# First projection of a two-layer hybrid encoder: x·r ahead, c and r in PSUM, other homes for some small work

## The chip, the cores and the metric

The kernel runs on one core of a Trainium2 chip. The metric is the device time of one execution in microseconds. Its engines are PE (matmul; PEld is its weight load), DVE (vector), ACT (scalar), POOL (GpSimd) and SP, which here only issues transfers.

## The reference

Batch 1, 512 positions, width 1024, two layers. Each layer is a token mixer with three groups of heads and then a gated MLP with a convolution of width 3. Everything is float32.

```python
for l in range(DEPTH):
    mod = jax.nn.silu(c) @ w_ada[l] + b_ada[l]
    sh_a, sc_a, gt_a, sh_f, sc_f, gt_f = [m[:, None, :] for m in jnp.split(mod, 6, axis=-1)]
    h = rms_norm(x, g_attn[l]) * (1.0 + sc_a) + sh_a
    x = x + gt_a * hybrid_mixer(h, w_in[l], diff_lambda[l], diff_subln[l], na_rpb[l], w_out[l], l)
    h = rms_norm(x, g_ffn[l]) * (1.0 + sc_f) + sh_f
    x = x + gt_f * conv_glu_ffn(h, w_up[l], conv_w[l], conv_b[l], w_down[l])
return rms_norm(x, g_final)
```

The mixer projects h to q, k and v for 4 differential heads (a softmax minus lambda times a second one), 6 dilated heads (three dilation patterns merged) and 6 heads of 2-D neighbourhood attention, with rope on the first two groups, and projects their outputs by w_out.

## The kernel before

x lies transposed: eight tiles of 128 features by 512 positions. For precision every matmul operand is split into a rounded part hi and a rest lo, and a product is three matmuls: hi·hi, lo (weight)·hi and hi·lo (`mm3`, L485 to L488). One such matmul is 128 x 128 by 512 columns.

**Weights** come in 110 units per layer, in the order of use. `emit_raw` (L323) loads one into a `raw` buffer (4 of them) on SP's queue; `emit_split` (L335) copies it to hi on ACT (L354) and takes lo = raw - hi on POOL or DVE (L355, L356). Three w slots hold split units (three more f slots in the MLP), so the split runs about one unit ahead of PE. `free_unit` gives a slot back and splits the next unit.

**Modulation.** Each column block of `mod` is one `ada_step` (L405): a 128 x 1024 block of w_ada times silu(c), which is copied to all partitions as `cb`, summed on DVE (L414), and for two of six groups a one-column product `gsc` = g·(1 + sc) (L421). 16 steps belong to the first projection, 24 run during layer 0's attention, the rest during its MLP.

**The start** (L201 to L232, L1297 to L1302): c arrives as two rows, silu on ACT, two matmuls against a row of ones, two copies to `cb`. x is loaded on SP. `Norm` squares x on ACT, sums seven squares on DVE (L447), and sums over partitions by eight one-column matmuls (L456); POOL takes the power (L461), four plus four small matmuls spread r over the partitions (L468).

**The first projection** is the generator `g0` (L500). For each of eight k-blocks it makes h (`make_h`, L472: x·r on DVE, L477; hi on ACT, L480; the affine step again on DVE, L481; lo on POOL in this place, L482), and then runs 18 matmuls into six PSUM banks (pr, pr, pr, pt, s, s). The same function serves the later normalised inputs.

**Attention** (`attention_phase`, L571). Rope pairs turn two banks into q and k parts (`rope_pair`, L587: four multiplications on DVE, then an add or subtraction, L606, a cast on ACT, L613, and lo, L618, these two on DVE or, where `G` is passed, on POOL), which go through DRAM scratch to be stacked. `proj()` (L774) is a generator that emits the remaining projections: V of the differential heads (`vd`), V of the dilated heads (`vb`), further q/k pairs, V of the third group, then w_out. `v_rows` (L664) and `v_split` (L702) write one bank per 128 positions, copy hi on ACT and take lo on DVE (L710), after which the bank is free. The main loop (L1106) takes one piece of `proj()`, advances a clock that runs due stages in order, and starts attention steps where their buffers are free; this sets the order in which instructions are emitted, and each engine works its list in order (a scheduler may move an instruction that is ready earlier). A differential step: scores, row maximum (L927), two exponentials (L935), reciprocal (L941), coefficient (L942), difference (L943), four transposes (L833), hi (L837) and lo (L841). A neighbourhood step scales its probabilities in L1031. w_out is split in two groups of units, o1 and o2.

**The MLP** (`ffn_phase`, L1137) is a long run of matmuls on the same weight machinery; its `Norm` adds squares on POOL.

PSUM has eight banks, 2 KB per partition each: pr 3, s 2, pt 2, o 1.

Of the kernel before, what the change touches and what calls it, by code (L numbers as in the profile page):

```python
# [176 lines left out]
def build(ctx, tc, a):  # L177
# [321 lines left out]

    def g0(l, kind, norm, rb0, A_off, sh_g):  # L500
        h = []
        first = l == 0 and kind == "g0"
        rb = {0: rb0}

        def mk(k, half):
            if half != 1:
# [1 line left out]
            if first and half != 1:
                with tc.issue_after(norm.last.ins):
                    ada_step()  # L510
                ada_step()
                if wst["raw"] < 8:
                    emit_raw()
                else:
                    wst["auto"] = True
# [854 lines left out]
```

## Time and profile before

| | us |
|---|---|
| median of 3 runs | 1367.7 (1364.79 to 1368.34) |
| the profiled execution | 1369.17 |
| its span, first to last instruction | 1367.4 |
| PE busy | 1290.9 (94%) |
| DVE busy | 918.2 (67%) |
| ACT busy | 607.3 (44%) |
| POOL busy | 178.1 (13%) |

In the profile, busy time is what an engine's instructions cover; a busy PE may still run its matmuls at half clock, so the granted clock is read beside it. Times in rows count from the first instruction. "L356" is line 356 of the kernel. In a group, the last part is the idle time of the engine ahead of the group's instructions and what ended it.

### The profile page before, as it was taken

The numbers are of one execution on the slowest core, as the hardware profiler recorded it, in microseconds if no ns is written. First come the engines' busy times: TensorE is split into PE (matmuls) and PEld (weight loads), VectorE is DVE, ScalarE is ACT, GpSimd is POOL, SyncE is SP. The second block draws the span as 40 slices with busy tenths as digits, with TensorE's granted clock in tenths as the row PEclk, the third lists the DMA queues.
The fourth block names the chain that finished last, engine by engine and source line by source line (L and its number), as shares of the span: only waits on it lengthen the run. The fifth ranks groups of instructions, "written<-read, shape, count | busy, mean of one in ns | idle before, by whom it ended". The sixth has DMA issues, their size and how long they took to land.

```text
span 1367.4 us, 18510 instructions
## 1 busy us (share of the span) xinstructions
PE 1290.9 (94%) x6860; PEld 1101.6 (81%) x6860; DVE 918.2 (67%) x1689; ACT 607.3 (44%) x1069; POOL 178.1 (13%) x116
## 2 busy tenths in 40 slices
PE   5887899897999999999999889999999999999997
PEld 4686689776988888888899867988898888888886
DVE  7968987797686666756666599579766434443443
ACT  3236578564443133313343467786645312331331
POOL 3732321003000000000022232200300000000002
PEclk9999999999999999999999999999999999999998
DMA  9556577755365656665532655475333233333211
GB/s 354 192 172 156 161 231 215 198 174 158 113 190 181 209 175 192 186 203 171 164 114 90 192 142 163 125 194 149 109 99 118 93 97 99 96 93 93 84 40 62
DMA packets 74861, 206.76 MB, mean 151 GB/s; under 512 B 8594, under 2 KB 12562, under 8 KB 74644
## 3 DMA queue, kind: packets, MB, share of 16 engines
q1 hardware_dynamic: 74048, 203.72, 49.7%
q10 hardware_dynamic: 724, 1.87, 0.4%
q8 instruction: 54, 0.88, 0.3%
q14 instruction: 35, 0.29, 0.1%
HBM read 180.39 MB, written 15.73 MB: 143 GB/s over the span
## 4 chain that ended last, share of the span: by engine, by line
PE 72%; DVE 14%; DMA 5%; ACT 3%; issue 3%; POOL 2%; SPq 0%; POOLq 0%; DVEq 0%; ACTq 0%
PE pr L488 10%; PE pr L487 9%; PE pr L486 9%; PE s L487 5%; PE s L486 5%; PE s L488 5%; PE pt L488 4%; PE pt L487 4%; PE pt L486 4%; PE o L487 2%; PE o L486 2%; PE o L488 2%; PE pt L833 2%; DMA raw<-w 2%; DVE tmp L414 2%
## 5 line engine op out<-in xcount | busy, mean ns | idle before, releaser
L354 ACT CAST whi<-raw 128x1024 fp32r<-128x1024 f32 (+2 forms) x144 | 134.8, 937 | 261.7 <-PE pr L488 97.3
L356 DVE TENSOR_TENSOR wlo<-raw,whi 128x1024 fp32r<-128x1024 f32 (+2 forms) x101 | 110.5, 1094 | 94.0 <-ACT whi L354 93.3
L447 POOL TENSOR_TENSOR tmp<-tmp,tmp 128x256 f32<-128x256 f32 (+1 forms) x38 | 36.6, 966 | 881.4 <-ACT tmp L445 880.4
L414 DVE CUSTOM_DVE_ANT_0 tmp<-raw,cb,par 128x1024 bf16<-128x1024 f32 x80 | 108.5, 1356 | 51.2 <-DMA raw<-w_ada 50.6
L354 ACT CAST fhi<-raw 128x1024 fp32r<-128x1024 f32 (+1 forms) x76 | 74.6, 985 | 143.6 <-PE pr L488 53.6
L488 PE MATMUL pr<-h,whi 128*128 128x512 f32 (+1 forms) x330 | 121.9, 374 | 8.2 <-POOL h L482 7.6
L356 POOL TENSOR_TENSOR wlo<-raw,whi 128x768 fp32r<-128x768 f32 (+1 forms) x43 | 97.2, 2266 | 232.1 <-ACT whi L354 190.3
L486 PE MATMUL pr<-h,whi 128*128 128x512 f32 (+1 forms) x330 | 124.0, 376 | 1.9 <-DVE tmp L599 1.0
L487 PE MATMUL pr<-h,wlo 128*128 128x512 f32 (+1 forms) x330 | 122.8, 373 | 1.3 <-POOL wlo L356 1.3
L356 DVE TENSOR_TENSOR flo<-raw,fhi 128x1024 fp32r<-128x1024 f32 (+1 forms) x76 | 87.0, 1147 | 54.6 <-ACT fhi L354 53.7
L486 PE MATMUL pr<-h,fhi 128*128 128x512 f32 (+1 forms) x244 | 86.8, 357 | 0.7 <-ACT h L480 0.7
L487 PE MATMUL pr<-h,flo 128*128 128x512 f32 (+1 forms) x244 | 86.4, 356 | 0.0
L488 PE MATMUL pr<-h,fhi 128*128 128x512 f32 (+1 forms) x244 | 85.6, 357 | 0.4 <-DVE h L482 0.4
L488 PEld LDWEIGHTS pr<-h,whi 128*128 128x128 f32 x330 | 62.1, 190 | 20.4 <-POOL h L482 10.3
L486 PEld LDWEIGHTS pr<-h,whi 128*128 128x128 f32 x330 | 62.8, 190 | 12.2 <-DVE tmp L599 1.7
L487 PEld LDWEIGHTS pr<-h,wlo 128*128 128x128 f32 x330 | 62.9, 191 | 10.5 <-POOL wlo L356 1.7
L1192 ACT ACTIVATE tmp<-tmp 128x512 f32<-128x512 f32 x44 | 27.6, 631 | 95.4 <-DVE tmp L1187 77.5
L927 DVE TENSOR_REDUCE sm<-s 128x1 f32<-128x512 f32 x64 | 43.0, 681 | 31.0 <-PE s L925 30.6
L837 ACT CAST ph<-pt 128x512 fp32r<-128x512 f32 x80 | 46.5, 582 | 35.8 <-PE pt L833 35.2
L841 DVE TENSOR_TENSOR pl<-pt,ph 128x512 fp32r<-128x512 f32 x80 | 54.2, 683 | 11.9 <-ACT ph L837 11.7
L833 PE MATMUL pt<-cst,tmp 128*128 128x128 f32 x320 | 48.9, 276 | 12.9 <-DVE tmp L943 9.5
L480 ACT ACTIVATE h<-tmp,mod,gsc 128x256 fp32r<-128x256 f32 (+1 forms) x58 | 34.8, 620 | 55.4 <-DVE tmp L477 54.6
(264 smaller groups left out, 3652.4 us busy)
## 6 DMA issues: line engine op xcount, KB each, us to landing
raw<-w SPq DMA_DIRECT2D x132, 512.0 KB
raw<-w_ada SPq DMA_DIRECT2D x80, 512.0 KB
raw<-w SPq DMA_DIRECT2D x72, 384.0 KB
araw<-w_ada SPq DMA_DIRECT2D x16, 512.0 KB
raw<-w SPq DMA_DIRECT2D x16, 320.0 KB
scr0b<-nat SPq DMA_DIRECT2D x12, 256.0 KB
qs<-nat SPq DMA_DIRECT2D x24, 128.0 KB
ks<-nat SPq DMA_DIRECT2D x24, 128.0 KB
```

What stands on the lines that cost most here:

```text
L354: A.copy(hi, r)
L356: (G if on_pool else V).tensor_tensor(out=lo, in0=r, in1=hi.bitcast(F32), op=ALU.subtract)
L414: V.tensor_tensor_reduce(out=junk, in0=r, in1=cb, op0=ALU.mult, op1=ALU.add, scale=1.0, scalar=par[:, OFF_B + l * 48 + j:OFF_B + l * 48 + ...
L447: self.last = self.eng.tensor_tensor(out=self.sq[0][:, sl], in0=self.sq[0][:, sl], in1=self.sq[m][:, sl], op=ALU.add)
L480: ins = A.activation(out=hi, in_=t, func=AF.Identity, scale=A_col, bias=sh_col)
L486: PE.matmul(out, wh, hh, start=first, stop=False)
L487: PE.matmul(out, wl, hh, start=False, stop=False)
L488: return PE.matmul(out, wh, hl, start=False, stop=last)
L833: PE.transpose(pt[:, kt], P[:, kt * 128:kt * 128 + 128], ident)
L837: A.copy(st["ph", half][:, :, sl], pt)
L841: V.tensor_tensor(out=st["pl", half][:, :, sl], in0=st["pt", qb], in1=st["ph", half][:, :, sl].bitcast(F32), op=ALU.subtract)
L927: V.tensor_reduce(out=nm[:, m:m + 1], in_=s, axis=AX.X, op=ALU.max, negate=True)
```

## The change

It has eight parts.

1. c comes by one broadcast transfer on ACT's queue; two Silu make `cx` (in PSUM, two banks) and `cb` (in SBUF). The first 16 `ada_step` read `cx`.
2. The first projection gets a generator of its own, `first_g0`. The transfers of ten w_ada blocks and five w_in units are issued first. The squares are all on ACT, five adds on DVE, three squares go to the statistics matmuls. r is spread into one bank, and x·r is one 512-wide DVE operation per block, for all blocks ahead of the matmuls. Both affine passes of h are on ACT, both lo parts on POOL. Matmuls run pass by pass over the banks (hi·hi for all, then the weight's lo, then h's lo). The sixth bank is the one that holds r.
3. `gsc` is made on ACT (Identity with scale and bias g).
4. V of the differential heads takes two PSUM banks of 512 columns for four position blocks; copy and lo are done once per bank. In layer 0 both are pt banks, and the fourth bank of the projection is o instead of pt.
5. Rope pairs b0, b1 and b2 do their add and lo on POOL.
6. The lo parts of o1 and o2, and of the first w_in unit, are on POOL.
7. The difference coefficient is one `tensor_scalar` with two scalar operands.
8. The neighbourhood steps scale on ACT.

```diff
+    cest = ExitStack()
+    cpp = cest.enter_context(tc.tile_pool(name="cpp", bufs=1, space=PSUM))
...
-    crow = [tmp((1, 512)) for _ in range(2)]
-    orow = tmp((1, 128))
-    V.memset(orow, 1.0)
-    for i in range(2):
-        A.dma_start(crow[i], a["c"][:, i * 512:i * 512 + 512])
+    cx = cpp.tile([128, D], F32, name="cx")
+    A.dma_start(cb, a["c"].broadcast_to([128, D]))
...
-    for i in range(2):
-        A.activation(out=crow[i], in_=crow[i], func=AF.Silu)
-        b = ps("s")
-        PE.matmul(b, orow, crow[i], start=True, stop=True)
-        A.copy(cb[:, i * 512:i * 512 + 512], b)
+    A.activation(out=cx, in_=cb, func=AF.Silu)
+    A.activation(out=cb, in_=cb, func=AF.Silu)
...
-        r = wp.tile([128, n], F32, tag="raw", bufs=4, name=f"raw{uid()}")
+        if l == 0 and u < 8:
+            r = fpool["p"].tile([128, n], F32, tag="graw", bufs=8, name=f"graw{uid()}")
+        else:
+            r = wp.tile([128, n], F32, tag="raw", bufs=4, name=f"raw{uid()}")
...
-        on_pool = (l == 0 and 0 < u < 8) or kind in ("b", "cq", "ck", "vc", "vb")
+        on_pool = (l == 0 and u < 8) or kind in ("b", "cq", "ck", "vc", "vb", "o1", "o2")
...
+        cv = cx if ada_st["n"] < 16 else cb
...
-            V.scalar_tensor_tensor(out=gsc[l][:, o + k:o + k + 1], in0=mod[l][:, j:j + 1], scalar=1.0,
-                                   in1=par[:, base + l * 8 + k:base + l * 8 + k + 1],
-                                   op0=ALU.add, op1=ALU.mult)
+            g = par[:, base + l * 8 + k:base + l * 8 + k + 1]
+            A.activation(out=gsc[l][:, o + k:o + k + 1], in_=mod[l][:, j:j + 1], func=AF.Identity, scale=g, bias=g)
...
+    def first_g0():
+        fp = fpool["p"]
+        for _ in range(5):
+            ada_load()
+            ada_load()
+            emit_raw()
+        sq = []
+        for k in range(KD):
+            sq.append(fp.tile([128, S], F32, tag="xt", bufs=8, name=f"xq{k}"))
+            A.activation(out=sq[k], in_=x[k], func=AF.Square)
+            if k in (2, 4, 5, 6, 7):
+                V.tensor_tensor(out=sq[0], in0=sq[0], in1=sq[k], op=ALU.add)
+        st = ps("s", (128, 4))
+        todo = [(k, j) for k in (1, 3, 0) for j in range(4)]
+        for i, (k, j) in enumerate(todo):
+            PE.matmul(st[:, j:j + 1], sq[k][:, j * 128:j * 128 + 128], ones, start=(i == 0), stop=(i == len(todo) - 1))
...
+        G.tensor_tensor(out=r, in0=v, in1=mh[:, 0:4], op=ALU.pow)
+        rb = ps("s")
+        for j in range(4):
+            PE.matmul(rb[:, j * 128:j * 128 + 128], r[:, j:j + 1].to_broadcast([128, 128]), ident, start=True, stop=True)
...
+        def norm_x(k):
+            xt.append(fp.tile([128, S], F32, tag="xt", bufs=8, name=f"xt{k}"))
+            V.tensor_tensor(out=xt[k], in0=x[k], in1=rb, op=ALU.mult)
+
+        def mk(k):
+            if wst["raw"] < 8:
+                emit_raw()
+            t = xt[k]
+            emit_split()
...
+            ins = A.activation(out=hi, in_=t, func=AF.Identity, scale=sc, bias=sh)
+            t2 = tmp()
+            A.activation(out=t2, in_=t, func=AF.Identity, scale=sc, bias=sh)
+            G.tensor_tensor(out=lo, in0=t2, in1=hi.bitcast(F32), op=ALU.subtract)
...
+        ada_step()
+        ada_step()
+        norm_x(0)
+        norm_x(1)
+        mk(0)
+        norm_x(2)
+        norm_x(3)
+        ada_step()
+        ada_step()
+        mk(1)
+        for k in range(4, KD):
+            norm_x(k)
+        banks = yield
...
+        def mms(k, cs):
+            wh, wl = us[k]
+            for w, m in ((wh, 0), (wl, 0), (wh, 1)):
+                for c in cs:
+                    PE.matmul(banks[c], w[:, c * 128:c * 128 + 128], h[k][m], start=(k == 0 and w is wh and m == 0),
+                              stop=(k == KD - 1 and m == 1))
+
+        for k in range(KD):
+            if k + 2 < KD:
+                ada_step()
+                ada_step()
+                mk(k + 2)
+            us[k] = next_unit(("g0", k))
+            if k == 0:
+                mms(0, range(5))
+            elif k == 1:
+                mms(1, range(5))
+                mms(0, (5,))
+                mms(1, (5,))
+                free_unit()
+            else:
+                mms(k, range(6))
+            if k:
+                free_unit()
+            ck.step()
+        cest.close()
+        late["pt"] = ctx.enter_context(tc.tile_pool(name="ppt", bufs=1, space=PSUM))
+        yield h
...
-        banks = [take(t) for t in ("pr", "pr", "pr", "pt", "s", "s")]
+        t3 = "pt" if l else "o"
+        banks = [take(t) for t in ("pr", "pr", "pr", t3, "s", "s")]
...
-                tags = ("pt", "o", "pr", "pr")
+                tags = ("pt", "pt", "o" if l else "pt", "o" if l else "pt")
...
+                if k == 0 and nu == 2 and tb % 2:
+                    outs[tb] = outs[tb - 1][:, n:2 * n]
...
-                rope_pair(("b", p), bk[0], bk[1], ("pr", "pr"), 1)
+                rope_pair(("b", p), bk[0], bk[1], ("pr", "pr"), 1, G)
...
-                V.scalar_tensor_tensor(out=r, in0=r, scalar=ld, in1=lamv[l][0], op0=ALU.mult, op1=ALU.mult)
+                V.tensor_scalar(out=r, in0=r, scalar1=ld, scalar2=lamv[l][0], op0=ALU.mult, op1=ALU.mult)
...
-                    V.tensor_scalar(out=P[:, cols[i]], in0=P[:, cols[i]], scalar1=dn[:, i:i + 1], scalar2=None,
-                                    op0=ALU.mult)
+                    A.activation(out=P[:, cols[i]], in_=P[:, cols[i]], func=AF.Copy, scale=dn[:, i:i + 1])
...
-        ck.after(2, lambda: rope_pair(("d", 1), banks[2], banks[3], ("pr", "pt"), 0, G))
-        ck.after(4, lambda: rope_pair(("b", 0), banks[4], banks[5], ("s", "s"), 1))
+        ck.after(2, lambda: rope_pair(("d", 1), banks[2], banks[3], ("pr", t3), 0, G))
+        ck.after(4, lambda: rope_pair(("b", 0), banks[4], banks[5], ("s", "s"), 1, G))
```

## Rows read from the trace of the kernel before

**Rows 1.** table by stretch: length, busy us per engine (instructions), clock, DMA share, GB/s

```profile
10.00:20.00 10.00, 3.94 (x16) 3.56 (x16) 6.60 (x12) 2.50 (x5) 2.06 (x1) 1.00 1.03 411
...
66.90:96.67 29.77, 24.51 (x157) 23.82 (x157) 19.84 (x30) 9.63 (x17) 13.64 (x8) 0.89 0.54 164
...
96.67:200.00 103.33, 90.95 (x483) 72.82 (x483) 93.30 (x179) 66.60 (x143) 28.36 (x12) 1.00 0.65 182
...
260.00:345.00 85.00, 70.79 (x421) 61.23 (x422) 73.23 (x192) 41.11 (x93) 11.54 (x13) 0.94 0.59 177
...
345.00:741.00 396.00, 395.59 (x2039) 337.34 (x2039) 261.90 (x403) 134.80 (x181) 11.15 (x10) 1.00 0.54 165
...
771.00:860.00 89.00, 81.67 (x439) 68.04 (x438) 77.58 (x153) 62.15 (x134) 24.46 (x12) 0.98 0.59 165
```

**Rows 2.** timeline, 10 to 21 us: start, length, engine, line [idle before, releaser]

```profile
10.78 0.69 DVE L443 TENSOR_TENSOR tmp<-x 128x512 f32<-128x512 f32 x1 [0.93 <-DMA x<-x]
...
13.65 1.86 PE L456 MATMUL pt<-cst,tmp 128*128 128x1 f32 x8 [3.84 <-DVE tmp L447]
...
20.27 0.58 PE L486 MATMUL pr<-h,whi 128*128 128x256 f32 x1 [0.29 <-ACT h L480]
```

**Rows 3.** chain of waits, 20 to 67 us: shares by line, one PE step

```profile
by line: POOL h L482 24.4%; POOL wlo L356 19.6%; DVE tmp L414 19.0%; issue 6.2%; PE pr L488 4.1%; ACT whi L354 4.0%; DVE tmp L477 3.7%; DVE tmp L481 2.9%; DVE gsc L421 2.9%; DVE tmp L599 2.7%; PE s L488 2.0%; PE s L487 1.9%; PE s L486 1.4%;
...
52.26 0.23 PE pr L487
```

**Rows 4.** single lines, whole span: ns min/median/max, first and last start

```profile
L482 POOL TENSOR_TENSOR h<-tmp,h x10: 722/1767/2349, 22.0 to 62.2; 128x512 fp32r<-128x512 f32 x6, 128x256 fp32r<-128x256 f32 x4
...
L356 POOL TENSOR_TENSOR wlo<-raw,whi x43: 1802/2387/2834, 23.5 to 893.7; 128x768 fp32r<-128x768 f32 x23, 128x1024 fp32r<-128x1024 f32 x20
...
L414 DVE CUSTOM_DVE_ANT_0 tmp<-araw,cb,par x16: 1271/1443/2919, 13.5 to 56.6; 128x1024 bf16<-128x1024 f32 x16
...
L481 DVE TENSOR_SCALAR tmp<-tmp,gsc,mod x58: 400/408/2064, 21.6 to 1008.3; 128x256 f32<-128x256 f32 x52, 128x512 f32<-128x512 f32 x6
...
L942 DVE SCALAR_TENSOR_TENSOR sm<-sm,sm,nl x32: 200/210/2392, 100.5 to 837.8; 128x1 f32<-128x1 f32 x32
```

**Rows 5.** groups by form, ACT, 20 to 67 us: busy us, mean ns

```profile
L480 ACT ACTIVATE h<-tmp,mod,gsc 128x512 fp32r<-128x512 f32 x6 | 4.9, 814 | 23.9 <-DVE tmp L477 23.9
```

**Rows 6.** timeline of PE, the two stages behind the first projections

```profile
86.25 0.69 PE L687 MATMUL pr<-whi,h 128*128 128x384 f32 x1 [3.87 <-DVE va L710]
...
760.48 0.69 PE L687 MATMUL pr<-whi,h 128*128 128x384 f32 x1 [3.86 <-DVE va L710]
```

**Rows 7.** timeline of POOL in layer 0's V stage

```profile
73.19 1.29 POOL L606 TENSOR_TENSOR tmp<-tmp,tmp 128x512 f32<-128x512 f32 x1
...
74.44 3.47 POOL L618 TENSOR_TENSOR nat<-tmp,nat 128x512 fp32r<-128x512 f32 x2
...
81.24 3.81 POOL L356 TENSOR_TENSOR wlo<-raw,whi 128x768 fp32r<-128x768 f32 x2 [3.33 <-ACT whi L354]
```

**Rows 8.** timeline, one differential step, 132 to 136 us

```profile
132.04 2.38 POOL L356 TENSOR_TENSOR wlo<-raw,whi 128x1024 fp32r<-128x1024 f32 x1 [11.33 <-DMA raw<-w]
...
132.26 2.17 DVE L942 SCALAR_TENSOR_TENSOR sm<-sm,sm,nl 128x1 f32<-128x1 f32 x1
...
134.47 0.75 DVE L943 SCALAR_TENSOR_TENSOR tmp<-tmp,sm,tmp 128x512 f32<-128x512 f32 x1
...
135.37 0.63 PE L833 MATMUL pt<-cst,tmp 128*128 128x128 f32 x4 [1.90 <-DVE tmp L943]
```

**Rows 9.** groups of DVE: first row 96 to 200 us, the others 250 to 345

```profile
L942 DVE SCALAR_TENSOR_TENSOR sm<-sm,sm,nl 128x1 f32<-128x1 f32 x16 | 10.5, 657 | 0.2
...
L1031 DVE TENSOR_SCALAR tmp<-tmp,sm 128x256 f32<-128x256 f32 (+1 forms) x24 | 7.0, 329 | 0.1
...
L356 DVE TENSOR_TENSOR wlo<-raw,whi 128x640 fp32r<-128x640 f32 (+1 forms) x12 | 10.9, 911 | 0.2 <-ACT whi L354 0.2
```

**Rows 10.** waits of PE, 200 to 345 us: total us, times, longest

```profile
PE pt L456 <- POOL tmp L447: 3.0, 1, 3.0
```

More of the change, by code (lines that the diff above doesn't have):

```diff
@@ L413, in ada_step @@
         junk = tmp((128, D), BF16)
-        V.tensor_tensor_reduce(out=junk, in0=r, in1=cb, op0=ALU.mult, op1=ALU.add, scale=1.0,
+        V.tensor_tensor_reduce(out=junk, in0=r, in1=cv, op0=ALU.mult, op1=ALU.add, scale=1.0,
                                scalar=par[:, OFF_B + l * 48 + j:OFF_B + l * 48 + j + 1],
@@ L498, in proj_cols @@
                 yield
+    def first_g0():
[14 more added lines that the diff above has]
+            PE.matmul(st[:, j:j + 1], sq[k][:, j * 128:j * 128 + 128], ones, start=(i == 0), stop=(i == len(todo) - 1))
+        v = tmp((128, 4), tag="sm4", bufs=4)
+        V.tensor_scalar(out=v, in0=st, scalar1=1.0 / D, scalar2=EPS, op0=ALU.mult, op1=ALU.add)
+        r = tmp((128, 4), tag="sm4", bufs=4)
+        G.tensor_tensor(out=r, in0=v, in1=mh[:, 0:4], op=ALU.pow)
+        rb = ps("s")
+        for j in range(4):
+            PE.matmul(rb[:, j * 128:j * 128 + 128], r[:, j:j + 1].to_broadcast([128, 128]), ident, start=True, stop=True)
+        xt, h = [], []
+        def norm_x(k):
[6 more added lines that the diff above has]
+            emit_split()
+            if k >= 1:
+                wst["auto"] = True
+            sc, sh = gsc[0][:, k:k + 1], mods(0, 0)[:, k:k + 1]
+            hi, lo = [wp.tile([128, S], F32R, tag="h", bufs=16, name=f"h{uid()}") for _ in range(2)]
+            h.append((hi, lo))
+            ins = A.activation(out=hi, in_=t, func=AF.Identity, scale=sc, bias=sh)
+            t2 = tmp()
+            A.activation(out=t2, in_=t, func=AF.Identity, scale=sc, bias=sh)
+            G.tensor_tensor(out=lo, in0=t2, in1=hi.bitcast(F32), op=ALU.subtract)
+            if k == 5:
+                with tc.issue_after(ins.ins):
+                    late_consts()
+        ada_step()
[11 more added lines that the diff above has]
+        banks = yield
+        us = {}
+        def mms(k, cs):
[25 more added lines that the diff above has]
+        yield h
@@ L507, in mk @@
                 h.append([wp.tile([128, S], F32R, tag="h", bufs=16, name=f"h{uid()}") for _ in range(2)])
[L508 to L515, printed above, removed]
-            ins = make_h(rb, k, half, gsc[l][:, A_off + k:A_off + k + 1], mods(l, sh_g)[:, k:k + 1], h[k],
-                         G if first else V)
-            if first and k == 5:
-                with tc.issue_after(ins.ins):
-                    late_consts()
-        if first:
-            seq = [(k, half) for k in range(2) for half in range(2)] + [(k, 2) for k in range(2, KD)]
-        else:
-            seq = sorted([(k + half * 3.5, k, half) for k in range(KD) for half in range(2)])
-            seq = [(k, half) for _, k, half in seq]
+            make_h(rb, k, half, gsc[l][:, A_off + k:A_off + k + 1], mods(l, sh_g)[:, k:k + 1], h[k], V)
+        seq = sorted([(k + half * 3.5, k, half) for k in range(KD) for half in range(2)])
+        seq = [(k, half) for _, k, half in seq]
         made = 0
@@ L535, in ahead @@
                 made += 1
-        if first:
-            for _ in range(3):
-                ada_load()
-                ada_load()
-                emit_raw()
-            emit_split()
-            emit_split()
-        ahead(1 if not first else 2)
+        ahead(1)
         banks = yield
@@ L548, in g0 @@
         for i, (k, half) in enumerate(seq):
-            if not first and i == 1:
+            if i == 1:
                 with tc.issue_after(ins.ins):
@@ L1295, in ffn_phase @@
         return norm, rb0, fest
-    norm = Norm(V, (0,))
     fest = open_f("s")
-    for m in range(KD):
-        norm.add(m, on_v=m == 7)
-    norm.stats(2)
-    rb0 = start_g0(0, "g0", norm, norm.bcast(0), 0, 0)
+    rb0 = first_g0()
+    next(rb0)
     for l in range(DEPTH):
```

37 lines of the change are left out of this document (21 added, 16 removed).

## The prediction

> **What bounds the kernel now.** Read first the table by stretch [rows 1]. In the middle (345 to 741 us, gate and up projections and the first down blocks) PE is busy 395.59 of 396 us: nothing this change does can shorten that work. What can go is idle time of PE, and it lies in five places: the first 67 us; the V projection behind it (granted clock 0.89, so PE also worked part of it at 1.2 instead of 2.4 GHz); the differential and first dilated steps (96.67 to 200 us, PE busy 90.95 of 103.33); the end of attention (260 to 345 us, 70.79 of 85); and layer 1's copy of the second and third place (771 to 860 us, 81.67 of 89).
>
> Next the chain of waits from 20 to 67 us [rows 3]. The projection's own work is 8 k-blocks x 6 banks x 3 = 144 matmuls, and one takes 0.23 us where PE runs without waiting: 33.1 us. It lasts from 20.27 [rows 2] to 66.9, where the stretch of V begins [rows 1]: 13.5 us are waits. The chain gives them to POOL (h L482 and wlo L356) and DVE (L414): PE's first line has 4.1%. The spread of single durations says why [rows 4]: the same POOL subtraction takes 1.80 or 2.83 us, L414 1.27 or 2.92, and L481, with one SBUF input, 0.40 or 2.06. DVE and POOL hold each other up when both read SBUF.
>
> **The change part by part.** *Before the first matmul.* The two rows of c, two K=1 matmuls and two copies go; c comes as one 0.52 MB broadcast on ACT's queue ahead of par and cst. At the 411 GB/s that 10 to 20 us show [rows 1] it costs the eight x loads beside it 1.3 us (0 to 2.6). SP then holds ten w_ada and five w_in loads instead of six and three; they stand behind x, so x loses nothing. Behind the last x, 13.65 - 10.78 = 2.9 us of DVE work become a Square on ACT and one add, about 1.3; of the twelve statistics matmuls only four wait for the last add, where eight did (1.86 us, so 0.9); the power on POOL and the broadcast of r stay; the first h block is 512 wide, not 256 (+0.5). Sum: 1.3 - 1.6 - 0.9 + 0.5 = -0.7. ACT could be later than x: it has two 1024-wide Silu (at most 3.3 us, four times the 0.81 of a 512-wide ACT operation [rows 5]) and eight Squares to do. I take the first matmul at 20 us (18.5 to 21.5).
>
> *The projection.* c now stands in PSUM, x·r reads PSUM, the affine step leaves DVE for a second ACT pass (0.81 us), and the tiny gain product leaves for ACT. DVE then runs nothing with two SBUF inputs and no tensor_scalar here, so its 16 L414 should take their shortest time, and so should POOL. Per k: POOL 1.80 + 1.3 (L482's shortest is 0.72 at 256 columns, its 512 columns go by L356's rate) = 3.1; DVE 2 x 1.27 + 0.16 = 2.7; ACT three passes, 2.6; DMA 1.44 MB at 411 GB/s, 3.5; PE 18 x 0.23 = 4.1. PE becomes the bound. The new order is hi·hi for all banks, then lo, so lo is due 1.1 us or more after hi. Two waits are added: bank 6 holds r, so it starts behind block 1; and DVE does x·r for four blocks ahead of w_ada rows 2 and 3 and four more ahead of rows 4 and 5, behind which ACT's h of blocks 1 and 2 waits. By that order h of block 2 is there at about 30.2 us where PE is free at 29.5. With 33.1 us of work, about 1 us for starting at 1.2 GHz and 1 us for this wait, the end is 20 + 35.1 = 55: **12 us** earlier than 66.9. Lower bound: if POOL kept its longest durations, 2.83 + 2.35 = 5.2 per k, 20 + 2 + 8 x 5.2 = 63.6, a gain of 3. Upper: first matmul at 18.5 and no wait, 14.
>
> *Diff V in two banks.* In layer 0 PE waited 3.87 us at 86.25 for a V subtraction on DVE to give a pr bank back; in layer 1 3.86 us [rows 6]. V now takes both pt banks (layer 1: pt and o), so the three pr banks come free with rope's four multiplications, long before. Layer 0 also spent 29.77 x 0.11 x 2 = 6.5 us at 1.2 GHz, where a matmul takes twice as long: 0 to 3.3 us of work, I take 1.7. So 5.6 us can go in layer 0 and, with a wait of the same length, as much in layer 1. Against that, rope pair b0 moves its two adds and two subtractions to POOL: 2 x 1.29 + 2 x 1.74 = 6.1 us [rows 7]. They stand in POOL's queue ahead of the lo of V-b units 1 and 2 (81.24 us), which PE needs some 4 us into V-b; POOL was idle 3.3 us there, so the lo comes 0 to 2.8 us later and PE waits 0 to 3.3. And the next stage is paced by DVE (93.30 of 103.33 us busy [rows 1]), so not all of what PE gains is kept. I take 3 us in layer 0 (0 to 7.2) and 2 in layer 1 (the same ends).
>
> *Difference coefficient.* In 96.67 to 200 us L942 costs 10.5 us for 16 one-element operations [rows 9]; at its median of 0.21 [rows 4] it would be 3.4, so 7 us are spent behind POOL. The pattern [rows 8]: POOL's subtraction (wlo) starts at 132.04, L942 at 132.26, both end at 134.4, and PE gets its transposes 1.90 us late. But L943 follows at once (134.47), depends on L942 and reads two SBUF tiles. Without the wait at L942 it meets the same subtraction: the wait moves one instruction down. Only where other DVE work stands between is time won. I count 2 of the 7 us in layer 0 (0 to 7) and 1 in layer 1.
>
> The form L942 is given has no row. Bounds: 0.2, and what a wider tensor_scalar shows when POOL is in the way, 2.06 [rows 4]; I take 0.2, since one element is nearer to L942's own short times. The Trainium skill (SBUF — State Buffer, "Who interferes with whom") says that tensor_scalar in a two-port mode takes the pair that DVE shares with POOL, and that whichever starts first keeps it for the whole instruction. L481's 2.06 agrees; by that rule the new form may wait as the old one did, these 3 us would be 0, and the time 1348.
>
> *b1 and b2 on POOL.* Two more pairs move in this stage: DVE loses 8 operations as wide as L943 (0.75 us [rows 8]), 6 us. POOL gains 2 x 6.1 = 12 us in the same 103, and each time it meets a DVE operation with two SBUF inputs, L943 or L414, one of the two waits. I take 1 us in layer 0 (-3 to 4), 1 in layer 1. Queued behind a POOL subtraction that waits for ACT's cast or for a store to free its buffer is the lo of the next weight unit, and behind that PE; the lead is one unit, 24 x 0.23 = 5.5 us.
>
> *Scaling on ACT, o1 and o2 lo on POOL.* DVE loses 24 L1031 (7.0 us) and 12 lo parts (10.9 us) per layer [rows 9]. In 260 to 345 us DVE is busy 73.23 of 85, but PE's longest explained wait there is for POOL's norm adds, 3.0 us [rows 10]. ACT gains 24 operations of 256 columns, 0.4 to 0.8 us each (half and all of the 512-wide 0.81 [rows 5]), 10 to 19 us beside 41 busy: hidden. POOL was busy 11.54: it takes 12 x 1.5 to 1.8 = 20 us, hidden behind 5 x 3 x 0.23 = 3.4 us of PE per unit, except o2, whose lo is 0.9 us slower and holds its raw buffer longer. I take 1 us in all (-5 to 6).
>
> **Sum.** 12 + 3 + 2 + 2 + 1 + 1 + 1 + 1 = 23 us. The profiled execution took 1369.2 us (span 1367.4): 1346.2; the median stands 1.5 us lower, so **1345**.
>
> **Rivals.** *Start only.* POOL takes back in attention what DVE loses (wait moved to L943, b0 ahead of V-b's lo). For it: [rows 7, 8]. Against: POOL is busy 28 of the 103 us up to 200 [rows 1]. Time: 1367.7 - 12 = 1356.
> *Start half.* The broadcast holds x up and ACT's ten operations come late, so that the first matmul is at 23, and x·r ahead of w_ada costs 3 us more: gain 6, with 5 of the rest 1357, alone 1362. Against: the last x, 2.1 MB in all, was there at 10.78 us, 200 GB/s on the mean, half of the 411 shown behind it; there is room for c.
> *Slower: POOL's queue.* Each rope pair puts 6.1 us ahead of a lo that PE needs. It decides from where POOL is behind by more than the 5.5 us lead: 6.1 is just over. If all six pairs cost PE 3 us, half clock after each stall 1, and o2 2 per layer, that is 28 against 12 + 8: 1376. Against: POOL has idle time ahead of most lo parts.
> *Nothing changes.* Only if DMA, not POOL, paced the projection; 1.44 MB per k at 411 GB/s is 3.5 us, under PE's 4.1. No chance of weight.
>
> **How the numbers follow.** Forecast 1345 (1335 to 1354): 0.52. Start only, 1354 to 1361: 0.24. Start half, 1356 to 1362: 0.12. More than forecast, under 1335 (the good ends are 14 + 7 + 7 + 7 + 4 + 6 against the 12 + 3 + 2 + 2 + 1 + 1 taken): 0.05. Slower, over 1368: 0.07, of which a part ends within 0.3%. The range 1333 to 1361 leaves out 0.2 at most. 0.3% (4 us) is about what a measurement of this kernel can tell from no change: faster 0.87, same 0.07, slower 0.06.
>
> **What would show it.** Right: L414 all near 1.28 before 55 us; POOL's two subtractions near 1.8 and 1.3; last matmul of the first projection near 55; no PE wait on a V subtraction in either layer; L942 all near 0.2, some L943 over 2. Wrong: POOL wlo ahead of PE in the V stage with over 3 us; the first matmul after 22; PE's idle time at 260 to 345 us grown; rope on POOL waiting for buffers with a lo behind it.

## The result, and the profile after

| kernel | median us | range | ratio to the kernel before, same chip (95% interval) |
|---|---|---|---|
| before | 1368.02 | 1364.79 to 1369.39 | |
| after | 1352.79 | 1349.55 to 1354.78 | 0.9887 (0.9866 to 0.9908) |
| forecast | 1345 | 1333 to 1361 | 0.983 |

The change made the kernel 15.2 us faster where 23 were forecast (1345, against the 1352.79 measured). The profiled execution of after took 1349.55 us (span 1347.8), the lowest of its range, that of before 1369.17, near the highest of its own; so the two differ by 19.6 us, and some 4 us of that are chance.

To see where the time went, both traces are cut at the same places of PE's own work: the cuts of before are those of [rows 1], 20.27 us (first matmul of the projection, [rows 2]) and 66.9 (where the V stage begins), and each cut of after is the moment at which PE has done the same amount of matmul work, added up from the trace's matmuls (to 0.4 us).

| stretch | before us | after us | gain | forecast |
|---|---|---|---|---|
| to the first matmul | 20.27 | 24.19 | -3.9 | 0.3 |
| first projection | 46.63 | 34.96 | 11.7 | 11.5 |
| V, layer 0 | 29.77 | 27.15 | 2.6 | 3 |
| differential and first dilated steps | 103.33 | 99.83 | 3.5 | 3 |
| rest of attention, layer 0 | 145.0 | 141.02 | 4.0 | about 1 |
| gate, up, first down blocks | 396.0 | 395.97 | 0.0 | 0 |
| V and steps, layer 1 | 119.0 | 114.35 | 4.7 | 4 |
| next 80 us, layer 1 | 80.0 | 79.57 | 0.4 | 0 |
| end of attention, layer 1 | 70.0 | 74.03 | -4.0 | 0 |
| to the end | 357.4 | 356.73 | 0.7 | 0 |

The kernel after, by these stretches (the columns are those of [rows 1]):

```profile
0.00:24.19 24.19, 7.53 (x33) 7.06 (x33) 7.90 (x17) 10.57 (x17) 5.24 (x7) 1.00 0.91 342
24.19:59.15 34.96, 34.96 (x147) 28.83 (x148) 23.76 (x39) 20.17 (x31) 21.17 (x14) 1.00 0.80 307
59.15:86.30 27.15, 24.07 (x158) 23.50 (x156) 15.22 (x25) 9.25 (x15) 18.17 (x12) 0.94 0.54 166
86.30:186.13 99.83, 89.51 (x483) 73.51 (x483) 85.03 (x171) 65.99 (x142) 38.55 (x20) 1.00 0.69 189
186.13:327.15 141.02, 130.35 (x787) 115.26 (x786) 107.94 (x266) 100.64 (x227) 40.87 (x29) 0.96 0.68 195
327.15:723.12 395.97, 395.56 (x2039) 337.59 (x2039) 260.70 (x387) 140.72 (x197) 11.14 (x10) 1.00 0.54 165
723.12:837.47 114.35, 105.70 (x606) 90.76 (x605) 83.67 (x165) 70.69 (x148) 54.10 (x32) 0.99 0.61 173
917.04:991.07 74.03, 69.80 (x468) 63.42 (x467) 55.25 (x128) 45.52 (x92) 23.31 (x20) 0.95 0.31 93
```

PE is busy for all 34.96 us of the projection: it became the bound, as forecast. Its first nine matmuls start 0.43 us apart and the others 0.23. In the steps behind V, DVE fell to 85.03 us from the 93.30 of [rows 1] and POOL rose to 38.55 from 28.36, yet PE's idle time fell only from 12.4 to 10.3 us.

*Ahead of the first matmul.* Timeline of after, columns as in [rows 2]:

```profile
11.10 1.40 SPq L403 DMA_DIRECT2D araw<-w_ada  x2
...
13.46 1.28 DVE L416 CUSTOM_DVE_ANT_0 tmp<-araw,cx,par 128x1024 bf16<-128x1024 f32 x1 [1.56 <-DMA araw<-w_ada]
...
14.67 0.69 DVE L512 TENSOR_TENSOR xq<-xq,xq 128x512 f32<-128x512 f32 x1
...
15.27 1.27 DVE L416 CUSTOM_DVE_ANT_0 tmp<-araw,cx,par 128x1024 bf16<-128x1024 f32 x1
...
16.47 0.69 DVE L512 TENSOR_TENSOR xq<-xq,xq 128x512 f32<-128x512 f32 x1
...
17.21 1.87 PE L516 MATMUL s<-cst,xq 128*128 128x1 f32 x8 [4.77 <-DVE xq L512]
...
24.19 1.65 PE L567 MATMUL pr<-h,whi 128*128 128x512 f32 x3 [1.69 <-ACT h L540]
```

DVE waits 1.56 us for a row of w_ada, with the last two adds of the statistics (L512) queued behind that product and the next. PE sits idle for 4.77 us before it can finish the statistics, and all that follows comes late with them.

*In the projection.* Single lines of after, 20 to 64 us (ns min/median/max, first and last start):

```profile
L416 DVE CUSTOM_DVE_ANT_0 tmp<-araw,cx,par x14: 1275/1278/1280, 24.9 to 43.0; 128x1024 bf16<-128x1024 f32 x14
L357 POOL TENSOR_TENSOR wlo<-graw,whi x7: 1832/1862/1877, 20.3 to 47.7; 128x768 fp32r<-128x768 f32 x7
L543 POOL TENSOR_TENSOR h<-tmp,h x8: 1283/1297/1311, 24.9 to 54.2; 128x512 fp32r<-128x512 f32 x8
```

None varies any more: 1.28, 1.86 and 1.30 us, where [rows 4] showed 1.27 to 2.92 and 1.80 to 2.83.

*In V of layer 0.* The waits for a V subtraction [rows 6] are gone; two others stand there (timeline of after):

```profile
71.56 0.62 ACT L683 CAST nat<-tmp 128x512 fp32r<-128x512 f32 x1 [3.59 <-POOL tmp L676]
...
73.45 1.28 ACT L249 ACT_TABLE_LOAD   x1
...
74.95 0.56 ACT L783 CAST va<-pt 128x512 fp32r<-128x512 f32 x1
...
75.41 2.30 ACT L355 CAST whi<-raw 128x768 fp32r<-128x768 f32 x3
...
76.30 0.44 PE L760 MATMUL pr<-whi,h 128*128 128x384 f32 x1 [1.63 <-ACT whi L355]
76.32 5.38 POOL L357 TENSOR_TENSOR wlo<-raw,whi 128x768 fp32r<-128x768 f32 x3 [1.06 <-DMA scr0d<-nat]
...
78.18 0.44 PE L761 MATMUL pr<-wlo,h 128*128 128x384 f32 x1 [1.45 <-POOL wlo L357]
```

PE waits first for ACT's cast of V-b's second weight unit, which stands in ACT's queue behind the casts of rope pair b0, the first of which had waited 3.59 us for POOL's sum, and behind a table load of 1.28 us; and then for POOL's lo.

*In the steps.* Timeline of after at 793 us (layer 1):

```profile
793.58 2.83 POOL L357 TENSOR_TENSOR wlo<-raw,whi 128x1024 fp32r<-128x1024 f32 x1
...
796.37 1.25 POOL L676 TENSOR_TENSOR tmp<-tmp,tmp 128x512 f32<-128x512 f32 x1
...
797.66 0.62 ACT L683 CAST nat<-tmp 128x512 fp32r<-128x512 f32 x1 [3.39 <-POOL tmp L676]
798.18 0.58 ACT L913 CAST ph<-pt 128x512 fp32r<-128x512 f32 x1
...
798.82 0.74 PE L930 MATMUL o<-ph,va 128*128 128x256 f32 x4 [2.72 <-ACT ph L913]
```

This chain is the new one of the kernel after: a rope sum on POOL stands behind a weight lo, ACT's cast of that sum waits 3.39 us for it, and the cast of the probabilities (ph), which depends on nothing there, stands behind that cast, and PE behind ph. Layer 0 has a like one at 136 us, where the sum takes 2.25 us beside a w_ada product of DVE instead of standing behind a lo, and PE waits 2.09 us for ph.

### The profile page after: what moved, and what is told of

It is laid out like the page before. It is cut to its first block, busy times and chain, and to the rows that moved or that the text cites. A ratio compares the mean times of both kernels' runs of the same rounds, so it can differ in the third digit from the quotient of the medians.

```text
span 1347.8 us, 18449 instructions
## 1 busy us (share of the span) xinstructions
PE 1285.7 (95%) x6836; PEld 1102.7 (82%) x6836; DVE 849.0 (63%) x1534; ACT 639.8 (47%) x1150; POOL 240.0 (18%) x163
## 4 chain that ended last, share of the span: by engine, by line
PE 72%; DMA 9%; DVE 7%; POOL 4%; issue 4%; ACT 3%; SPq 1%; POOLq 0%; DVEq 0%; ACTq 0%
PE pr L489 9%; PE pr L488 9%; PE pr L487 9%; PE s L488 5%; PE s L487 5%; PE s L489 5%; PE pt L488 4%; PE pt L489 4%; PE pt L487 4%; PE o L488 2%; PE o L489 2%; PE o L487 2%; PE pt L909 2%; DMA raw<-w 1%; PE pr L567 1%
## 5 line engine op out<-in xcount | busy, mean ns | idle before, releaser
L355 ACT CAST whi<-raw 128x1024 fp32r<-128x1024 f32 (+2 forms) x136 | 128.1, 943 | 229.6 <-PE pr L489 78.2
L357 POOL TENSOR_TENSOR wlo<-raw,whi 128x768 fp32r<-128x768 f32 (+2 forms) x58 | 115.0, 1988 | 299.4 <-ACT whi L355 275.4
L357 DVE TENSOR_TENSOR wlo<-raw,whi 128x1024 fp32r<-128x1024 f32 (+1 forms) x78 | 90.8, 1164 | 101.4 <-ACT whi L355 100.6
L487 PE MATMUL pr<-h,whi 128*128 128x512 f32 (+1 forms) x300 | 113.2, 378 | 0.4 <-DVE tmp L669 0.4
L489 PE MATMUL pr<-h,whi 128*128 128x512 f32 (+1 forms) x300 | 111.5, 372 | 0.4 <-DVE h L483 0.4
L488 PE MATMUL pr<-h,wlo 128*128 128x512 f32 (+1 forms) x300 | 111.7, 372 | 0.0
L917 DVE TENSOR_TENSOR pl<-pt,ph 128x512 fp32r<-128x512 f32 x80 | 54.6, 685 | 18.0 <-ACT ph L913 17.7
L489 PEld LDWEIGHTS pr<-h,whi 128*128 128x128 f32 x300 | 56.7, 189 | 9.5 <-DVE h L483 0.6
L487 PEld LDWEIGHTS pr<-h,whi 128*128 128x128 f32 x300 | 56.8, 189 | 8.9 <-DVE tmp L669 0.7
L488 PEld LDWEIGHTS pr<-h,wlo 128*128 128x128 f32 x300 | 56.9, 190 | 8.7 <-POOL wlo L357 0.6
L909 PEld LDWEIGHTS pt<-cst,tmp 128*128 128x128 f32 x320 | 37.7, 140 | 19.8 <-issue 5.9
```

The source lines that it names most:

```text
L355: A.copy(hi, r)
L357: (G if on_pool else V).tensor_tensor(out=lo, in0=r, in1=hi.bitcast(F32), op=ALU.subtract)
L487: PE.matmul(out, wh, hh, start=first, stop=False)
L488: PE.matmul(out, wl, hh, start=False, stop=False)
L489: return PE.matmul(out, wh, hl, start=False, stop=last)
L909: PE.transpose(pt[:, kt], P[:, kt * 128:kt * 128 + 128], ident)
```

## The experiments

Every kernel was timed beside the kernel before on the same chip; one ratio is uncertain by 0.002 (3 us), a difference of two by about 0.003 (4 us). After was timed a second time for this:

> The kernel after, unchanged, beside the others of this set, since differences of 2 to 6 us are to be read against it on the same chip. Theory (the gain is 15 us, the 2/3 of the 23 forecast): ratio to the kernel before 0.987 to 0.990. Rival (the profiled gain of 19 us is the usual one): 0.985 to 0.987.

It gave 0.9902 (0.9882 to 0.9922), so 14.4 us (0.9895) is taken for after below. Its second profiled execution had a span of 1354.6 us, 6.8 more than the first, with the same program: 3.1 us of that lie in the differential steps of layer 0 and 3.3 in those of layer 1. Its differential steps of layer 0:

```profile
87.14:190.08 102.94, 92.68 (x483) 76.06 (x483) 83.56 (x169) 66.23 (x142) 38.09 (x20) 0.97 0.66 187
```

PE's idle time there is 10.3 us in both traces; the granted clock is 0.97 instead of 1.00. Of the gains of 3.5 and 4.7 us that the table above shows in the steps of layer 0 and in V and steps of layer 1, this trace keeps 0.4 and 1.3. What differs by less than 3 us between two traces in these steps is no evidence. Another limit: most edits make the program that orders the queues choose another order elsewhere, on PE too. PE's order stayed the same in 2, 8 and 10. In 2 and 8 nothing moved behind the first projection; in it, besides what the edit names, some operations of ACT and subtractions of POOL changed places.

**1. The start alone.** The kernel after with the four edits of experiments 3, 4, 6 and 7 and that of 12 together.

> The new start alone (c in PSUM, x.r up front, scaling on ACT, lo on POOL in the first projection), with V bank by bank, the coefficient, the rope pairs, the NA scaling and the o1/o2 lo parts as in the kernel before. Theory (the start gave 8 of the profiled 19 us, since the last matmul of the first projection came at 58.8 instead of 66.9, and attention the rest): about 1360 us, 8 under the kernel before and 7 over the kernel after; PE waits about 3.9 us again for a V subtraction in both layers. Rival, start only (what attention saves, POOL takes back): about 1353, as the whole change.

1362.07 us, 0.9942 (0.9925 to 0.9959): 7.9 us, the theory's 8; PE's waits for a V subtraction are back with 5.0 us in layer 0 and 3.9 in layer 1. So the start gave 8 and attention the other 6 of the 14.

**2. The order ahead of the first matmul.**

```diff
-                V.tensor_tensor(out=sq[0], in0=sq[0], in1=sq[k], op=ALU.add)
+                last = V.tensor_tensor(out=sq[0], in0=sq[0], in1=sq[k], op=ALU.add)
...
-        ada_step()
-        ada_step()
+        with tc.issue_after(last.ins):
+            ada_step()
+            ada_step()
```

> The kernel after with one thing changed: the first two w_ada products stand behind the last add of squares on DVE instead of between the adds. Theory (the two products, 1.28 us each with a wait of 1.56 us for the w_ada row ahead of them, held the statistics up by 3.9 us): last add at about 13.3 instead of 17.2, first matmul at 20.3 to 21.5 instead of 24.2, last matmul of the first projection at 55 to 56 instead of 58.6; time 2.5 to 3.5 us under the kernel after, about 1350. Rival (ACT, the weights or the w_ada rows are late, so that the statistics were not what mattered): first matmul not before 23.5 or, if it is earlier, waits inside the projection that let it end at 58 all the same; time as the kernel after, about 1353.

1349.22 us, 0.9852 (0.9832 to 0.9873), 5.9 under after, above the theory's 2.5 to 3.5 but not by more than the uncertainty. Its timeline:

```profile
10.46 3.08 DVE L512 TENSOR_TENSOR xq<-xq,xq 128x512 f32<-128x512 f32 x4 [0.35 <-ACT xq L510]
...
13.60 1.87 PE L516 MATMUL s<-cst,xq 128*128 128x1 f32 x8 [1.10 <-DVE xq L512]
13.64 1.28 DVE L416 CUSTOM_DVE_ANT_0 tmp<-araw,cx,par 128x1024 bf16<-128x1024 f32 x1
...
20.58 1.65 PE L568 MATMUL pr<-h,whi 128*128 128x512 f32 x3 [1.69 <-ACT h L540]
```

The last statistics start at 13.60 instead of 17.21, the first matmul at 20.58, the last of the projection starts at 54.6 instead of 58.6. The theory holds: what held the statistics up were two products of 1.28 us in DVE's queue, with a wait of 1.56 us for a row, and not x, ACT or the weights.

**8. Where c stands.**

```diff
-        cv = cx if ada_st["n"] < 16 else cb
+        cv = cb
```

> The kernel after with the 16 w_ada products of the first projection reading c from SBUF instead of PSUM; nothing else differs, also not in the order. Theory (DVE and POOL hold each other up where both read SBUF with two inputs): the products, 1.27 to 1.28 us in the kernel after, take up to 2.9 again, POOL's lo parts (1.83 to 1.87 and 1.29 to 1.31) up to 2.8 and 2.1; the last matmul of the first projection comes 1 to 5 us later than 58.6; time 1 to 4 us slower. Rival (what made both slow before were the other DVE operations, and the projection has slack now): products and POOL's parts keep their times or grow without PE waiting; last matmul at 58.6 still, time the same within 1 us.

1363.77 us, 0.9971 (0.9955 to 0.9987): 9.4 slower than after beside it, more than the theory's 1 to 4. The same lines as above, and PE's waits up to 70 us:

```profile
L416 DVE CUSTOM_DVE_ANT_0 tmp<-araw,cb,par x14: 1271/2302/2891, 26.0 to 56.2; 128x1024 bf16<-128x1024 f32 x14
L357 POOL TENSOR_TENSOR wlo<-graw,whi x7: 2825/2857/2863, 27.2 to 57.9; 128x768 fp32r<-128x768 f32 x7
L543 POOL TENSOR_TENSOR h<-tmp,h x8: 1277/2069/2279, 26.0 to 62.9; 128x512 fp32r<-128x512 f32 x8
...
PE pr L567 <- POOL h L543: 5.0, 4, 3.3
PE pr L567 <- ACT h L540: 2.9, 3, 1.7
```

The edit is one operand's place. DVE's and PE's order is the same; on ACT two casts and on POOL two subtractions changed places, so the expectation's "also not in the order" doesn't hold in full. The product rises from 1.28 to a median of 2.30 us, POOL's lo from 1.86 to 2.86, and the last matmul of the projection starts at 69.97 instead of 58.6; 1.1 us of that are there at the first matmul already (25.28). So c's place, with these changes of order, is worth about all of the 7.9 us that the start gained in experiment 1; without it 4 us are left of the whole change. The Trainium skill (SBUF — State Buffer, "Who interferes with whom") says that a DVE instruction with at most one SBUF input, outside the two-port modes, does not contend with GpSimd; the 1.28 against 2.30 us agree.

**11 and 3. The difference coefficient,** alone in the kernel before, and taken back in the kernel after (the edit of 11; 3 is its reverse):

```diff
-                V.scalar_tensor_tensor(out=r, in0=r, scalar=ld, in1=lamv[l][0], op0=ALU.mult, op1=ALU.mult)
+                V.tensor_scalar(out=r, in0=r, scalar1=ld, scalar2=lamv[l][0], op0=ALU.mult, op1=ALU.mult)
```

> The kernel before with one thing changed: the coefficient of the difference in its new form. Theory (the wait for POOL moves one instruction down): the 32 coefficients take 8.5 us instead of 17.7, the 32 differences 31 to 34 instead of 25.9, 2 to 4 us net on DVE; time 0 to 4 us under the kernel before, 1364 to 1368. Rival (the form is worth what its return cost in the kernel after, 6 us or more): 1362 or less.

> The kernel after with the coefficient of the difference back in its old form (one element, the second factor as a tensor). Theory (the wait for POOL only moves one instruction down): the 32 coefficients take 17 to 18 us instead of 8.5 in all, the 32 differences behind them about 26 instead of 33.3, so 1 to 2 us net over both layers; time 0 to 2 us over the kernel after, 1353 to 1355. Rival (the wait is gone for good and the longer differences have another cause): differences stay at 33, time 7 to 9 us over the kernel after, about 1361.

Experiment 11: 1363.30 us, 0.9956 (0.9938 to 0.9975), 5.9 us faster than before (3.4 to 8.5). Experiment 3: 1361.45 us, 0.9928 (0.9909 to 0.9946), 4.5 slower than after. Groups of DVE, whole span, first in the kernel before, then in 11, then in after:

```profile
L943 DVE SCALAR_TENSOR_TENSOR tmp<-tmp,sm,tmp 128x512 f32<-128x512 f32 x32 | 25.9, 808 | 0.3
L942 DVE SCALAR_TENSOR_TENSOR sm<-sm,sm,nl 128x1 f32<-128x1 f32 x32 | 17.7, 554 | 0.2
```

```profile
L943 DVE SCALAR_TENSOR_TENSOR tmp<-tmp,sm,tmp 128x512 f32<-128x512 f32 x32 | 33.5, 1046 | 0.2
L942 DVE TENSOR_SCALAR sm<-sm,sm,nl 128x1 f32<-128x1 f32 x32 | 8.5, 266 | 0.2
```

```profile
L1019 DVE SCALAR_TENSOR_TENSOR tmp<-tmp,sm,tmp 128x512 f32<-128x512 f32 x32 | 33.3, 1040 | 0.2
L1018 DVE TENSOR_SCALAR sm<-sm,sm,nl 128x1 f32<-128x1 f32 x32 | 8.5, 265 | 0.2
```

In 11 the coefficients lose 9.2 us and the differences gain 7.6: the wait moved one instruction down, as the theory says, and 1.6 us of DVE remain. The time fell by more than that, between the theory's 0 to 4 and the rival's 6, and in 3 it rose by more than the theory's 0 to 2. In 3 the coefficients take 13.9 us and the differences 30.5, less than the 17 to 18 and more than the 26 of its theory. PE's waits for a difference, whole span, fell from 9.5 to 7.8 us from before to 11 and rose from 7.0 to 11.2 from after to 3, in 3 about as much as the time. The traces don't settle why: in both builds other DVE instructions changed places as well (in 3 the subtraction pl moved ahead of a V subtraction), and 11's own trace has PE only 2.0 us ahead of before at the end.

**4, 9 and 10. The rope pairs.** Pairs b0, b1, b2 back on DVE (4, and 9 with the order of 2), and only b0 back (10, with the order of 2):

```diff
-                rope_pair(("b", p), bk[0], bk[1], ("pr", "pr"), 1, G)
+                rope_pair(("b", p), bk[0], bk[1], ("pr", "pr"), 1)
...
-        ck.after(4, lambda: rope_pair(("b", 0), banks[4], banks[5], ("s", "s"), 1, G))
+        ck.after(4, lambda: rope_pair(("b", 0), banks[4], banks[5], ("s", "s"), 1))
```

> The kernel after with the adds and subtractions of rope pairs b0, b1 and b2 back on DVE. Theory (pair b0 on POOL holds up ACT's cast and POOL's lo of the second V-b unit in layer 0; b1 and b2 relieve DVE a little): PE's waits of 1.6 and 1.4 us at the second V-b unit go, which gives 3 us there, and the differential steps lose 1 to 3 us; net between 2 us faster and 1 us slower than the kernel after. Rival 1 (POOL's queue is what eats the gain in attention): 4 us or more faster, 1349 or less. Rival 2 (DVE paces the steps up to 200 us, so its 18 us per layer count): 4 us or more slower.

> The kernel after with two things: the first two w_ada products behind the last add of squares, and the adds and subtractions of rope pairs b0, b1, b2 back on DVE. Theory (both losses are real and lie in different places): first matmul at 20.6, no wait at the second V-b unit, 4 us from the first and 2 to 6 from the second: ratio to the kernel before 0.980 to 0.985, 1340 to 1348 us, the fastest so far. Rival (what V gains, the differential steps take back whenever they start earlier, since they are paced by DVE): ratio as with the order alone, 0.985 to 0.988.

> As the run before it, but only pair b0 goes back to DVE; b1 and b2 stay on POOL. Theory (only b0 stands ahead of V-b's weights; b1 and b2 on POOL relieve DVE where it paces): the wait at the second V-b unit is gone here too, and the differential steps lose less, so it is 0 to 3 us faster than with all three on DVE. Rival (b1 and b2 on POOL hold DVE's own two-input operations up as long as they would take on it): the same within 1.5 us, or slower by up to 3.

| | median us | ratio (95% interval) |
|---|---|---|
| after | 1352.79, 1354.05 | 0.9887, 0.9902 |
| 4: b0, b1, b2 on DVE | 1348.84 | 0.9840 (0.9819 to 0.9862) |
| 2: order | 1349.22 | 0.9852 (0.9832 to 0.9873) |
| 10: order, b0 on DVE | 1351.02 | 0.9860 (0.9840 to 0.9880) |
| 9: order, b0, b1, b2 on DVE | 1342.38 | 0.9805 (0.9783 to 0.9827) |

Experiment 4 is 7.5 us faster than after, the rival that POOL's queue eats the gain. 9 is 7.5 faster than 10, and 10 no faster than 2: it is b1 and b2 that cost, and my expectation for 10, that only b0 stands in the way, fell. ACT's waits from 86 to 860 us (total, times, longest) in before, after and 9, and PE's waits from 723 to 837 us, first in after, then in 9 (721 to 833):

```profile
ACT nat L613 <- POOL tmp L606: 1.9, 2, 1.3
```

```profile
ACT nat L683 <- POOL tmp L676: 22.1, 12, 3.4
...
PE pt L909 <- DVE tmp L1019: 4.0, 3, 2.3
PE o L930 <- ACT ph L913: 2.7, 1, 2.7
```

```profile
ACT nat L684 <- POOL tmp L677: 3.0, 2, 2.0
...
PE pt L910 <- DVE tmp L1020: 3.7, 2, 2.3
PE s L1002 <- DMA qs<-scr1d: 1.4, 2, 1.2
```

ACT's wait for POOL's rope sums rose from 1.9 to 22.1 us and falls to 3.0 with the pairs on DVE, and with it PE's wait of 2.7 us for ph goes. In the steps of layer 0 PE waits 3.7 us for ph in 10 and 0.7 in 9 (78 to 186 and 78 to 184 us), first 10, then 9:

```profile
PE o L931 <- ACT ph L914: 3.7, 3, 2.2
PE s L1002 <- DMA qs<-scr0d: 3.5, 2, 2.3
```

```profile
PE o L931 <- ACT ph L914: 0.7, 1, 0.7
```

Over both layers that is 6.4 us in 10 against 0.7 in 9, most of the 7.5. PE's order differs between these two as well, so the share of ACT's wait is read from the waits and not shown alone. b0 differs: in 4 both waits at V-b go. From 2 to 10, where only b0 moves and PE's order stays, V falls from 27.1 to 22.0 us, but the steps behind it rise from 101.7 to 108.0, and 10 is no faster than 2. In part that is a new wait: in 10 PE waits 3.5 us for the transfer of the rope output that comes back through DRAM (second line above), which 2 doesn't show.

**12. Diff V.** Bank by bank again:

```diff
-                tags = ("pt", "pt", "o" if l else "pt", "o" if l else "pt")
+                tags = ("pt", "o" if l else "pt", "pr", "pr")
```

> The kernel after with the V of the differential heads again bank by bank, two token blocks in the pr banks (in layer 0 the first two in both pt banks). Theory (the banks are worth 2 to 6 us in each layer where PE waited for a V subtraction): a wait of 3 to 4 us comes back at the first V-b unit of layer 1 (about 740 us) and one of 2 to 4 in layer 0 (72 to 77 us), of which 2 to 4 us in all reach the end; time 2 to 6 us over the kernel after. Rival (what V gains is taken back by the steps behind it, 5 us of 6.5 in layer 1 by the end of attention): the waits come back but the time stays within 1.5 us of the kernel after.

1362.85 us, 0.9952 (0.9934 to 0.9970), 7.8 slower than after: above the theory's 2 to 6, though not by more than the uncertainty, and the rival (1.5) is out. In layer 0 the old wait returns (PE's waits, 60 to 90 us):

```profile
PE pr L758 <- DVE va L782: 4.1, 2, 3.4
```

In layer 1 the waits that return at V are 0.4 us for DVE and 2.0 for POOL's lo, less than expected, and further ones of the steps grow (3.9 us for ph, in place of 2.7).

**6 and 7. Scaling, and the lo parts of o1 and o2,** back on DVE:

```diff
-                    A.activation(out=P[:, cols[i]], in_=P[:, cols[i]], func=AF.Copy, scale=dn[:, i:i + 1])
+                    V.tensor_scalar(out=P[:, cols[i]], in0=P[:, cols[i]], scalar1=dn[:, i:i + 1], scalar2=None, op0=ALU.mult)
```

```diff
-        on_pool = (l == 0 and u < 8) or kind in ("b", "cq", "ck", "vc", "vb", "o1", "o2")
+        on_pool = (l == 0 and u < 8) or kind in ("b", "cq", "ck", "vc", "vb")
```

> The kernel after with the scaling of the neighbourhood probabilities back on DVE (24 operations a layer). Theory (ACT's queue is late with the casts ph in layer 1's last steps, where PE now loses 3.4 us at 920 to 930 us and 1.9 at 960 to 970 us that it did not lose before): PE's wait at 923 us for the second product of a neighbourhood head goes or falls under 0.5 us, 2 to 4 us faster than the kernel after. Rival 1 (the lo parts of o1 and o2 on POOL make that wait): it stays at 1.8 us, time within 1.5 us of the kernel after. Rival 2 (DVE needs the relief): DVE's 7 us per layer come back as PE waits in 250 to 330 us, 2 us or more slower.

> The kernel after with the lo parts of o1 and o2 back on DVE (12 a layer, 0.8 to 1 us each there). Theory (hidden on POOL, in the way on DVE): DVE +11 us per layer between 200 and 330 us and in the same stretch of layer 1; layer 0 loses 0 to 3 us, because PE's waits there ended on DVE and on POOL's norm adds; the wait at 923 us in layer 1 stays; time 0 to 4 us slower than the kernel after. Rival (POOL's lo parts of o1 and o2 are what PE waits for in layer 1, or hold its raw buffers): 2 us or more faster.

1353.77 us (0.9895) and 1354.04 (0.9897), against 0.9902 beside them: no difference. In 6 this is two differences that cancel. Cut at equal work of PE, the rest of layer 0's attention and the end of layer 1's in 6:

```profile
188.60:334.10 145.50, 129.35 (x785) 114.05 (x785) 116.17 (x291) 92.70 (x202) 43.09 (x29) 0.96 0.65 188
925.60:995.30 69.70, 66.26 (x467) 60.62 (x466) 56.45 (x139) 40.71 (x80) 23.29 (x20) 1.00 0.31 93
```

The two traces of after take 141.0 and 141.2 us for the first and 74.0 and 72.5 for the second. So scaling on ACT gains 4 us in layer 0 and loses 3 to 4 in layer 1, where PE's order is the same in 6 as in after: this is the 4.0 us that the end of layer 1's attention lost. All four kernels that scale on DVE (before, 1, 6 and 11) take 68.9 to 70.0 us there, at a granted clock of 1.00, and the ten traces that scale on ACT 72.5 to 74.2. Most of the loss is clock: for the same work PE is busy 69.80 us in after, at 0.95, and 66.26 in 6. The wait that the theory of 6 blamed isn't the way: PE's wait for the neighbourhood product at 923 us (1.5 us for pl in after) is there with 1.2 us in 6. How scaling on ACT brings the lower clock stays open. In 7 PE's waits for pl sum to 3.8 us, and the end of layer 1 keeps its 73.4.

## Why the prediction was right and where it was not

The time lay in the range, and about two thirds of the forecast gain came. But the terms were less right than their sum, and that the sum came near is in part luck: errors of both signs cancel. Each part by its experiment (differences of 4 us uncertainty):

| part | forecast us | measured us |
|---|---|---|
| start | 12 (3 to 14) | 7.9 (experiment 1) |
| diff V | 5 | 7.8 (12) |
| coefficient | 3 | 5.9 in before (11), 4.5 in after (3) |
| rope on POOL | 2 | -7.5 (4; b1 and b2 alone, 9 against 10, the same) |
| scaling, o1 and o2 lo | 1 | -1.0 and -0.7 (6, 7), nothing measurable in sum |
| sum | 23 | 11 to 12, where after showed 14 to 15.2 |

*Before the first matmul: the step that failed.* The prediction put it at -0.7, the first matmul at 20, and looked for a late ACT or a late x. It was 24.19. The sum counted one add behind the last x and left out what else DVE has in its queue there: two w_ada products that don't belong to the statistics, with the wait for their row. Experiment 2 moved them and got 20.58, inside the 18.5 to 21.5. Even there the 1.6 us that the sum took off for the adds didn't come: four adds stand in a row up to 13.54 us, and in the kernel before the last statistics started at 13.65 [rows 2]. The sign that the prediction named as wrong (first matmul after 22) was there; its cause was not one of those it named for *start half*.

*The projection: right, in size and cause.* Forecast 35.1 us from the first matmul to the end, found 34.6 (the first matmul of V starts at 58.82). The two terms beside the work were off in opposite ways: the start at 0.43 us a matmul cost about 2 us where 1 was taken, and the wait for h of block 2, also taken as 1, didn't come. L414's successor at 1.28, POOL at 1.86 and 1.30 for 1.8 and 1.3. Experiment 8 showed that c in PSUM does it.

*Diff V: right place, too small.* The wait for a V subtraction went in both layers [rows 6]. The price of 0 to 3.3 us for pair b0 was met at its upper end (1.63 + 1.45), but half of it came through ACT's queue, which the prediction did not look at. The two stretches show 2.6 us for layer 0; experiment 12 puts 7.8 of the whole on V.

*Coefficient: mechanism right, price too low in us.* The wait moved to the next instruction: 7.6 of 9.2 us in experiment 11. The form took 0.25 to 0.28 us each time, never a wait, against the 0.2 taken. In the prediction the Trainium skill's rule (SBUF — State Buffer, "Who interferes with whom") was read to mean that this tensor_scalar may wait for the shared pair as the old form did; on one element it did not, in any of its 32 instances, so the 1348 had no ground here. What the end gained above the 1.6 us of DVE is open.

*b1 and b2 on POOL: wrong sign, and the largest error.* The step read POOL's queue and DVE's: it asked what stands behind a POOL subtraction on POOL and who contends with it. It did not ask who on ACT waits for it. On POOL the sum stands behind a lo of 2.83 us, and ACT, which works in order, holds ph and so PE behind the cast of that sum. The rival *slower: POOL's queue* had the direction of this (each pair puts 6.1 us into a queue that PE needs) but the wrong follower, the weight's lo, and came to 28 us in all; the pairs cost 7.5.

*Scaling and lo parts: right in sum, by luck.* The prediction had the scaling hidden on ACT. It gained about 4 us in layer 0 and cost 3 to 4 at the end of layer 1 (experiment 6), and neither was forecast. The lo parts are worth nothing measurable.

The rival *start only* would have had the rest worth nothing; experiment 1 leaves 6.5 us for it. *Start half* gave about the right size for the start (6, measured 7.9) for the wrong reason.

With both losses taken out (order, and rope of b0 to b2 on DVE, experiment 9) the kernel runs at 1342.38 us, 26.8 under the kernel before, close to the forecast of 23.

## What to carry to other kernels

An operation that moves to an idle engine must be followed one engine further: list who reads its result, and what stands in order behind that reader; here POOL had the time for 62 us more, but the rope sums among them made ACT wait 20 us, with PE's operands behind it. An edit that shows no difference can hold a gain and a loss: cut both traces at equal work before calling a part worth nothing. When a chain is shortened, read what else the scheduler can slip into the queues it runs through, and tie that down, which was worth 4 us at the front. Where DVE and POOL run two-input work side by side, try one operand in PSUM; here it freed both.
